# Context projections of a DeltaNet layer: float32 products of unsplit weights in place of three fp32r products of split ones

## The chip, the core and the metric

The kernel runs on one core of one Trainium2 chip. The metric is the device time of one execution in microseconds, as the median of several runs; a lower one is better. The core has TensorE (PE in the rows; its weight loads are PEld), VectorE (DVE), ScalarE (ACT), GpSimd (POOL) and SyncE (SP), which here only issues DMAs. Each engine works through its own list of instructions in order and waits on semaphores.

## The reference, cut to what matters

A layer of a diffusion backbone: gated DeltaNet attention over 512 latent tokens, whose scans start from the final states of scans over 256 context tokens, then a retrieval mixer (PEER) with 128 blocks of 128 experts. D is 1024, there are 8 heads of 128.

```python
hn  = _modulate(_rmsnorm(h, norm_g[i, 0]), sh1, sc1)            # 512 latent tokens
hcn = _modulate(_rmsnorm(hc, norm_g[i, 0]), modc[0], modc[1])   # 256 context tokens
...
z = hn @ w_in                     # the same w_in for both streams
qkv = jax.nn.silu(_short_conv(z[..., :3 * DN_INNER], conv_w, n_rows))
ba = z[..., 4 * DN_INNER:].astype(jnp.float32).reshape(B, L, 2, 2, DN_HEADS)
...
_, sc_f = _gated_delta_chunked(kc, vc, betac[:, 0], gc[:, 0], s0, None)   # context: k, v, decays
o_f, _ = _gated_delta_chunked(k, v, beta[:, 0], g[:, 0], sc_f, q)         # latent, seeded
```

Everything is float32. Of the context only k and v are needed, so its projections are 8 heads of k and 8 of v: a product of a 1024x128 slice of `w_in` with the 1024x256 normed context for each.

## The kernel before, in words

The projections are a list of jobs, one for each head and kind: jobs 0 to 7 are context k (`ck`), 8 to 15 context v (`cv`), and from 16 on the latent q, k, v and gate. A loop over t runs them as a pipeline: in step t it does the projection of job t (`Pj`), the conv taps of job t-1 (`taps`, L353: ACT makes the centre tap, DVE four more, reading the projection from PSUM), transposes and copies of job t-2, fills with pieces of block inverses and norms, splits the weights of job t+2 and loads those of job t+3. Jobs 0 to 3 are done ahead of the loop, chunk by chunk as the context norm comes out (`norm_c`).

A projection multiplies in three fp32r products for each of its 8 chunks of 128 rows. The weight tile `w` (128x1024, 512 KB, DMA by SP) is split into a high part `wh` (cast to fp32r by ACT, L325) and a low part `wl` (`w - wh` by POOL, L326); the normed context is split in the same way into `hcx` high (ACT, L233) and low (DVE, L243). The products are high by high, high by low, low by high (L333), 128x128 weights on 128x256 for the context and on 128x512 for the latent stream. The buffers of `w` are two (WB[0]), those of `wh` and `wl` three each (WB[1]); job 3 splits into two halves in other buffers (`w3`). A projection's result stands in one of two PSUM buffers `pz`; ahead of the loop jobs 2 and 3 use `pk`.

Beside each chunk of the context norm stands a small float32 product for the decays (`aux<-wba,hn`, L247). When its last chunk is done, ACT copies it (`ba`, L260), and a chain of small operations on DVE and ACT makes the decays `g_c`; rows built from them by DVE and POOL (`rw`, L382) go through PE (L396 in fp32r, L399 in float32, both 128x256) into the matrices `Nc`.

Which instruction stands where on an engine is set by the tile framework, which follows the order of the code with priorities, and by buffers that come free. A DMA into a buffer is issued when the last reader of its former content is done.

Of the kernel before, what the change touches and what calls it, by code (L numbers as in the profile page):

```python
# [9 lines left out]
F32 = mybir.dt.float32  # L10
F32R = mybir.dt.float32r
# [4 lines left out]
OP = mybir.AluOpType  # L16
# [4 lines left out]
P = 128  # L21
D = 1024
NC = D // P
TL = 512
TC = 256
H = 8
# [29 lines left out]
WB = (2, 3)  # L56
# [5 lines left out]
NB = {'hn': 4, 'acc': 2, 'ko': 2, 'st': 2}  # L62
# [49 lines left out]
class Trunk:  # L112
# [104 lines left out]
    def norm_rs(self, st, T, rs=None):  # L217
# [3 lines left out]
        nc.vector.reciprocal(rs[:, :T], rs[:, :T])  # L221
        return rs

    def norm_hi(self, src, rs, T, s_, hi, c):
        nc, ma = self.nc, self.ma
        hn = self.tmp("hn", "hn", NB["hn"])
        if NM & (1 + s_):
            nc.vector.scalar_tensor_tensor(hn[:, :T], src[:, c, :], ma[:, c, 1, s_:s_ + 1], rs[:, :T], op0=OP.mult, op1=OP.mult)
            nc.scalar.activation(hi[:, c, :], hn[:, :T], AF.Identity, bias=ma[:, c, 0, s_:s_ + 1])
            return hn  # L230
        (nc.gpsimd if s_ == 0 and c in NP[0] else nc.vector).tensor_tensor(hn[:, :T], src[:, c, :], rs[:, :T], op=OP.mult)
        nc.vector.tensor_scalar(hn[:, :T], hn[:, :T], ma[:, c, 1, s_:s_ + 1], ma[:, c, 0, s_:s_ + 1], op0=OP.mult, op1=OP.add)
        nc.scalar.copy(hi[:, c, :], hn[:, :T])  # L233
        return hn
# [79 lines left out]
        res.update(beta=bt, eG=ex[:, 0], kds=ex[:, 1], gl=ex[:, 2], neg=neg)  # L314


    def w_load(self, src):
        w = self.wp.tile([P, NC, P], F32, name="w", tag="w", bufs=WB[0])
        self.nc.sync.dma_start(w, src)
        return w  # L320

# [7 lines left out]
    def products(self, z, src, w, T):  # L329
        wh, wl = w  # L330
        for c in range(NC):
            for n, (w_, x_) in enumerate(((wh, 0), (wh, 1), (wl, 0))):
                self.nc.tensor.matmul(z[:, :T], w_[c // 4][:, c % 4, :] if isinstance(w_, list) else w_[:, c, :], src[x_][:, c, :], start=c + n == 0, stop=c == NC - 1 and n == 2)  # L333
            yield

    def project(self, src, w, T):
# [266 lines left out]
    def run(self):  # L603
        nc, a, C, mod, ng, dram, tc = self.nc, self.a, self.C, self.mod, self.ng, self.dram, self.tc
        with ExitStack() as tk:
# [43 lines left out]
            for i in (1, 0):  # L649
                nc.vector.tensor_tensor(dg[:, i], C["ident"][:, None, :].to_broadcast([P, NC, P]), self.c2[:, :, i:i + 1].to_broadcast([P, NC, P]),  # L650
                                        op=OP.mult)
# [7 lines left out]
            rsc = self.norm_rs(st_, TC)  # L659
            self.wba = self.cst.tile([P, NC, 32], F32, name="wba")  # L660
            nc.sync.dma_start(self.wba, a["wba"])
            hcx = self.tp.tile([P, 2, NC, TC], F32R, name="hcx", tag="big", bufs=1)
            hc = (hcx[:, 0], hcx[:, 1])
            knc = ub.tile([P, 2, H, P], F32, name="knc")
            vc = ub.tile([P, 2, H, P], F32, name="vc")
            Ncv = Nc.rearrange("p (d t h) i -> p d t h i", d=2, t=2)
# [20 lines left out]
            def load(n):  # L687
                if n < nj:
                    kind, h = jobs[n]
                    ws[n] = self.w_load(a["w_in"][col[kind] + h])  # L690
                elif n < nj + NO:
                    ws[n] = self.w_load(a["w_out"][n - nj])

            def split(n):
                if n < nj + NO:
                    ws[n] = self.w_split(ws[n])

            def Pj(n):
                kind, h = jobs[n]
                g, T, rows, nt = geo(kind)  # L700
                st[n]["z"] = self.project(hc if kind[0] == "c" else hl, ws.pop(n), T)

            def taps(n):
                kind, h = jobs[n]
# [81 lines left out]

            load(0)
            load(1)
            split(0)
            split(1)  # L790
            load(2)
            self.load_params()
            load(3)
            rows = knc.rearrange("p t h d -> p (t h d)")[0:2, :].rearrange("p (i x) -> p i x", x=512)
            bac = self.psum("aux", 1)
            hn = {}
            z0 = [self.pz(), self.pz()]
            pr = []

            def norm_c(cs, last):  # L800
                for c in cs:
                    hn[c] = self.norm_hi(xc, rsc, TC, 1, hc[0], c)
                    if c - 1 in hn:
                        self.norm_lo(hn.pop(c - 1), TC, hc[0], hc[1], bac, c - 1)
                        for p in pr:
                            next(p)
                if last:
                    self.norm_lo(hn.pop(7), TC, hc[0], hc[1], bac, 7)
                    for p in pr:
                        next(p)  # L810
                        next(p, None)

            self.mods_rows(0, ada[0], rows)
            self.mods_rows(1, ada[1], rows)
            self.mods_turn(rows)
            z0.append(self.pk())
            for n in range(3):
                st[n]["z"] = z0[n]
                if n == 2:
                    split(n)  # L820
                pr.append(self.products(z0[n], hc, ws[n], TC))
            norm_c(range(4), False)
            junk = vc.rearrange("p t h d -> p (t h d)")[:, :D]
            self.mods_dots(adaT, cb2, 1, junk)
            norm_c(range(4, 8), True)
            wp = [[self.tmp("w3", "st", NB["st"], (P, 4, P), F32R) for _ in range(2)] for _ in range(2)]
            for i in range(2):
                self.w_split(ws[3][:, 4 * i:4 * i + 4, :], [wp[n][i] for n in range(2)])
            ws[3] = wp
            st[3]["z"] = self.pk()  # L830
            for _ in self.products(st[3]["z"], hc, ws[3], TC):
                pass
            for c in range(NC):
                nc.sync.dma_start(xT[:, c, :], a["xT"][:, c, :])
            load(4)
# [50 lines left out]
            for t in range(1, nj + 3):  # L886
# [57 lines left out]
                        silu(t - 1)  # L944
                with prio("split"):
                    split(t + 2) if t >= 3 else None
                if t == 2:
                    split(4)
                if t <= nj:
                    B(t - 1)  # L950
                mk = []
# [813 lines left out]
```

## Time and profile before

| | |
|---|---|
| median of 3 runs | 1951.41 us (1949.15 to 1956.68) |
| the profiled execution | 1956.64 us |
| its span, first to last instruction | 1954.9 us |
| PE busy over the span | 1819.3 us (93%) |
| DVE busy | 1562.8 us (80%) |
| ACT busy | 855.1 us (44%) |
| POOL busy | 625.6 us (32%) |
| first context product to the last | 41.75 to 151.3 us |
| first latent product | 152.92 us |

Times in the rows are microseconds from the first instruction, means of one instruction are in ns. PE's busy time is modelled from overlapping products, so what a product costs is read from the distance of two starts. A float32 product is recorded as two halves, an fp32r product as one. L12 is line 12 of the kernel.

### The profile page before, as it was taken

What the parts mean: (1) busy time and instruction counts of PE and PEld (TensorE: products, weight loads), DVE (VectorE), ACT (ScalarE), POOL (GpSimd) and SP (SyncE); (2) the same over time, 40 slices, a digit from 0 to 9 for tenths busy, and PEclk for the clock granted to TensorE, in tenths of its full rate; (3) what the DMA queues carried; (4) which work ended last, traced back from release to release, by engine and by line L of the source; (5) the groups of instructions that cost most, each with busy time, mean ns of one, the idle gap of its engine ahead of it and who ended that gap; (6) DMA issues with size and microseconds to landing.
All of it is one profiled execution on the core that took longest, in us unless ns stands there. A gap on an engine that the chain in (4) does not pass through costs nothing.

```text
span 1954.9 us, 29971 instructions
## 1 busy us (share of the span) xinstructions
PE 1819.3 (93%) x11119; PEld 1609.9 (82%) x11119; DVE 1562.8 (80%) x3267; ACT 855.1 (44%) x1399; POOL 625.6 (32%) x395
## 2 busy tenths in 40 slices
PE   7778899878998899799999999999999999999997
PEld 4776788766898887689999888788999998889996
DVE  5998967979388789978999687777777887777885
ACT  3655634523445243247666533333333333333333
POOL 1544412361001133321111022333444443434433
PEclk8888879988799899899999999999999999999998
DMA  8221346424635532147999989999989988989981
GB/s 307 67 87 54 87 130 207 133 86 146 190 114 179 177 98 87 55 162 265 308 316 316 327 292 321 323 346 323 314 311 326 334 304 311 328 304 318 325 275 64
DMA packets 202274, 440.65 MB, mean 225 GB/s; under 512 B 15504, under 2 KB 103696, under 8 KB 198800
## 3 DMA queue, kind: packets, MB, share of 16 engines
q1 hardware_dynamic: 155472, 269.87, 42.5%
q0 software_dynamic: 36864, 134.23, 19.4%
q10 hardware_dynamic: 9792, 34.64, 4.4%
q8 instruction: 87, 1.43, 0.3%
q14 instruction: 59, 0.48, 0.1%
HBM read 388.88 MB, written 49.81 MB: 224 GB/s over the span
## 4 chain that ended last, share of the span: by engine, by line
PE 51%; DVE 11%; DMA 5%; issue 1%; SPq 1%; ACT 0%; DVEq 0%; ACTq 0%
PE pz L1232 25%; PE y L1574 21%; PE py L1509 2%; DMA hTt<-hT_d 2%; DMA ge<-pre_d 2%; DVE wk L1350 1%; PE pz L333 1%; DVE keys L1353 1%; DVE keys L1352 1%; DVE row L1288 1%; DVE keys L1349 1%; DVE keys L1351 1%; DVE wl L1603 1%; DMA keys<-G_d 0%; PE pk L1106 0%
## 5 line engine op out<-in xcount | busy, mean ns | idle before, releaser
L1232 PE MATMUL pz<-hH,wh 128*128 128x384 f32 (+1 forms) x1128 | 391.6, 347 | 2.5 <-ACT small L1253 2.5
L1232 PE MATMUL pz<-hH,wl 128*128 128x384 f32 (+1 forms) x1128 | 389.2, 345 | 0.0
L1232 PE MATMUL pz<-hL,wh 128*128 128x384 f32 (+1 forms) x1128 | 388.8, 345 | 0.0
L1280 POOL DMA_INDIRECT row<-u,small x128 | 169.0, 1320 | 478.3 <-DVE row L1288 456.1
L1597 ACT CAST wh<-w 128x1024 fp32r<-128x1024 f32 x196 | 205.4, 1054 | 181.7 <-PE y L1574 98.0
L1603 DVE TENSOR_TENSOR wl<-w,wh 128x1024 fp32r<-128x1024 f32 x196 | 240.4, 1227 | 46.5 <-ACT wh L1597 46.3
L1280 POOL DMA_INDIRECT row<-v,small x128 | 180.2, 1408 | 223.1 <-DVE small L1296 204.8
L326 POOL TENSOR_TENSOR wl<-w,wh 128x1024 fp32r<-128x1024 f32 x53 | 149.0, 2814 | 294.6 <-ACT wh L325 291.2
L1574 PE MATMUL y<-wh,ch 128*128 128x512 f32 x768 | 238.6, 392 | 2.8 <-ACT ch L1560 2.8
L1574 PE MATMUL y<-wh,cl 128*128 128x512 f32 x768 | 238.0, 391 | 1.8 <-DVE cl L1561 1.8
L1574 PE MATMUL y<-wl,ch 128*128 128x512 f32 x768 | 237.7, 391 | 0.0
L1232 PEld LDWEIGHTS pz<-hH,wh 128*128 128x128 f32 x1128 | 213.6, 189 | 9.5 <-ACT small L1253 2.9
L1232 PEld LDWEIGHTS pz<-hL,wh 128*128 128x128 f32 x1128 | 213.4, 189 | 6.4 <-issue 0.2
L1232 PEld LDWEIGHTS pz<-hH,wl 128*128 128x128 f32 x1128 | 213.2, 189 | 4.3
L1574 PEld LDWEIGHTS y<-wh,cl 128*128 128x128 f32 x768 | 144.2, 188 | 33.4 <-DVE cl L1561 2.8
L1574 PEld LDWEIGHTS y<-wl,ch 128*128 128x128 f32 x768 | 144.5, 188 | 31.4
L1574 PEld LDWEIGHTS y<-wh,ch 128*128 128x128 f32 x768 | 143.5, 188 | 28.9 <-ACT ch L1560 3.5
L1296 DVE SCALAR_TENSOR_TENSOR small<-row,small 128x1024 f32<-128x1024 f32 x127 | 162.6, 1280 | 1.2
L1288 DVE SCALAR_TENSOR_TENSOR row<-row,small 128x1024 f32<-128x1024 f32 x128 | 155.2, 1219 | 0.0
L1253 ACT ACTIVATE ge<-pz 128x384 f32<-128x384 f32 x108 | 53.5, 495 | 214.1 <-PE pz L1232 212.8
L333 PE MATMUL pz<-hlH,wh 128*128 128x512 f32 x256 | 112.4, 439 | 24.4 <-DVE acc L353 19.8
L1516 ACT ACTIVATE keys<-py 128x512 f32<-128x512 f32 x96 | 105.0, 1093 | 55.7 <-PE py L1509 50.8
(477 smaller groups left out, 3361.0 us busy)
## 6 DMA issues: line engine op xcount, KB each, us to landing
w<-uT SPq DMA_DIRECT2D x128, 512.0 KB, 5.0
w<-v SPq DMA_DIRECT2D x128, 512.0 KB, 5.1
w<-w_in SPq DMA_DIRECT2D x48, 512.0 KB, 3.7
G_d<-keys ACTq DMA_DIRECT2D x24, 1024.0 KB, 6.5
adaw<-adaT SPq DMA_DIRECT2D x64, 256.0 KB, 3.4
keys<-G_d SPq DMA_DIRECT2D x8, 1536.0 KB, 13.5
Gt<-G_d SPq DMA_DIRECT2D x8, 1536.0 KB, 13.8
w<-w_q SPq DMA_DIRECT2D x16, 512.0 KB, 3.7
```

Of the source, the lines that this page charges most:

```text
L326: self.last_split = (eng or nc.gpsimd).tensor_tensor(wl, w, wh.bitcast(F32), op=OP.subtract)
L333: self.nc.tensor.matmul(z[:, :T], w_[c // 4][:, c % 4, :] if isinstance(w_, list) else w_[:, c, :], src[x_][:, c, :], start=c + n == 0, st ...
L1232: self.nc.tensor.matmul(out, w[i][:, c, :], x_[:, c, sl], start=c == 0 and n == 0, stop=c == NC - 1 and n == 2)
L1253: self.nc.scalar.activation(ge, z, AF.Gelu)
L1280: nc.gpsimd.indirect_dma_start(out=r, out_offset=None, in_=a["u"] if k < P else a["v"], in_offset=bass.IndirectOffsetOnAxis(ap=self.idx[:, ...
L1288: nc.vector.scalar_tensor_tensor(r, r, 1.0, self.xg, op0=OP.mult, op1=OP.mult, accum_out=self.hid_g[:, k:k + 1])
L1296: nc.vector.scalar_tensor_tensor(self.yg, r, self.coef[:, k:k + 1], self.yg, op0=OP.mult, op1=OP.add)
L1509: nc.tensor.matmul(gp[:, r * P:(r + 1) * P], e[:, 2 + r // 2, :, r % 2], oa[:, 2 * w + r // 2, :, r % 2], start=r == 0 and w == 0, stop=w ...
L1516: nc.scalar.activation(Gs[:, :, i * 4:i * 4 + 4].rearrange("p a t -> p t a"), gps.pop(p).rearrange("p (t a) -> p t a", t=4), AF.Copy, scal ...
L1574: nc.tensor.matmul(yp[2 * t + hf], c_[:, t * P:(t + 1) * P], v_[:, hf * 512:hf * 512 + 512], start=b == 0 and w == 0, stop=b == NBLK - 1 a ...
L1597: nc.scalar.copy(wh, w)
L1603: nc.vector.tensor_tensor(wl, w, wh.bitcast(F32), op=OP.subtract)
```

## The change

The 16 context jobs multiply in float32: one product for each chunk, from the weights as loaded and from the norm as computed. The norm (`norm_whole`) writes float32 straight into `hcx`, without a cast and a subtraction. The weights of the context jobs are not split; they are loaded into the buffers of `w`, `wh` and `wl` in turn (job number modulo 3). Jobs 0 to 3 all go chunk by chunk with the norm. The latent jobs keep their three products, and their splits are as before.

```diff
+    def norm_whole(self, src, rs, h, ba_ps, c):
+        nc, ma = self.nc, self.ma
+        nc.vector.tensor_tensor(h[:, c, :], src[:, c, :], rs[:, :TC], op=OP.mult)
+        nc.vector.tensor_scalar(h[:, c, :], h[:, c, :], ma[:, c, 1, 1:2], ma[:, c, 0, 1:2], op0=OP.mult, op1=OP.add)
+        for t in range(TC // P):
+            nc.tensor.matmul(ba_ps[:, t * 32:(t + 1) * 32], h[:, c, t * P:(t + 1) * P], self.wba[:, c, :], start=c + t == 0,
+                             stop=c == NC - 1, skip_group_check=True)
...
-    def w_load(self, src):
-        w = self.wp.tile([P, NC, P], F32, name="w", tag="w", bufs=WB[0])
+    def w_load(self, src, i=0):
+        w = self.wp.tile([P, NC, P], F32, name="w", tag=("w", "wh", "wl")[i], bufs=WB[i > 0])
...
+    def whole(self, z, src, w):
+        for c in range(NC):
+            self.nc.tensor.matmul(z[:, :TC], w[:, c, :], src[:, c, :], start=c == 0, stop=c == NC - 1)
             yield
...
-            hcx = self.tp.tile([P, 2, NC, TC], F32R, name="hcx", tag="big", bufs=1)
-            hc = (hcx[:, 0], hcx[:, 1])
+            hc = self.tp.tile([P, NC, TC], F32, name="hcx", tag="big", bufs=1)
...
-                    ws[n] = self.w_load(a["w_in"][col[kind] + h])
+                    ws[n] = self.w_load(a["w_in"][col[kind] + h], n % 3 if kind[0] == "c" else 0)
...
-                if n < nj + NO:
+                if 2 * H <= n < nj + NO:
                     ws[n] = self.w_split(ws[n])
...
-                st[n]["z"] = self.project(hc if kind[0] == "c" else hl, ws.pop(n), T)
+                if kind[0] == "c":
+                    st[n]["z"] = self.pz()
+                    for _ in self.whole(st[n]["z"], hc, ws.pop(n)):
+                        pass
+                else:
+                    st[n]["z"] = self.project(hl, ws.pop(n), T)
...
             load(0)
             load(1)
-            split(0)
-            split(1)
             load(2)
...
-            z0 = [self.pz(), self.pz()]
+            z0 = [self.pz(), self.pz(), self.pk(), self.pk()]
...
-                    hn[c] = self.norm_hi(xc, rsc, TC, 1, hc[0], c)
-                    if c - 1 in hn:
-                        self.norm_lo(hn.pop(c - 1), TC, hc[0], hc[1], bac, c - 1)
...
+                    self.norm_whole(xc, rsc, hc, bac, c)
                     for p in pr:
                         next(p)
...
-            for n in range(3):
+            for n in range(4):
                 st[n]["z"] = z0[n]
-                if n == 2:
-                    split(n)
-                pr.append(self.products(z0[n], hc, ws[n], TC))
-            norm_c(range(4), False)
+                pr.append(self.whole(z0[n], hc, ws[n]))
+            norm_c(range(4))
...
-            wp = [[self.tmp("w3", "st", NB["st"], (P, 4, P), F32R) for _ in range(2)] for _ in range(2)]
-            for i in range(2):
-                self.w_split(ws[3][:, 4 * i:4 * i + 4, :], [wp[n][i] for n in range(2)])
...
-                if t == 2:
-                    split(4)
```

On POOL, from its first arithmetic on (`wl` and `w_381` are low parts of weights, `rs` sums for the latent norm, `rw` rows of the context decays), there stood before:

```order
L326 TENSOR_TENSOR wl<-w,wh 128x1024 x3
L326 TENSOR_TENSOR w_381<-w,w_379 128x512
L912 TENSOR_TENSOR rs<-sq 128x512
L912 TENSOR_TENSOR rs<-rs,sq 128x512 x2
L382 TENSOR_TENSOR rw<-cbuf,g_c 128x256 x2
L326 TENSOR_TENSOR w_382<-w,w_380 128x512
L326 TENSOR_TENSOR wl<-w,wh 128x1024
```

And in the changed kernel (its L335 is the split, L397 the rows, L240 a product of the latent norm):

```order
L912 TENSOR_TENSOR rs<-sq 128x512
L912 TENSOR_TENSOR rs<-rs,sq 128x512 x3
L397 TENSOR_TENSOR rw<-cbuf,g_c 128x256 x8
L240 TENSOR_TENSOR hn<-xT,rs 128x512
L335 TENSOR_TENSOR wl<-w,wh 128x1024 x3
```

The sixteen context splits are gone, and the first three that are left belong to latent jobs 16 to 18.

On PE, at the end of the jobs ahead of the loop, there stood before (L247 is the decay projection, `pk<-hcx,w_379` job 3, L304 the sums of the decays):

```order
L247 MATMUL aux<-wba,hn 128x32 x5
L333 MATMUL pk<-hcx,wh 128x256 x2
L247 MATMUL aux<-wba,hn 128x32
L333 MATMUL pz<-hcx,wh 128x256 x2
L247 MATMUL aux<-wba,hn 128x32 x2
L333 MATMUL pk<-hcx,wl 128x256
```

And in the changed kernel (L230 is the decay projection, L348 a float32 product, L916 the sum for the latent norm, L313 the sums of the decays):

```order
L230 MATMUL aux<-wba,hcx 128x32 x2
L348 MATMUL pz<-hcx,w 128x256 x2
L348 MATMUL pk<-hcx,w 128x256 x2
L916 MATMUL aux<-rs,cbuf 128x512
L348 MATMUL pz<-hcx,w 128x256 x5
L313 MATMUL pk<-gd__356,cbuf 128x16
```

The last decay product, which stood ahead of most products of job 2 and of all of job 3, now stands behind all but the last chunk of jobs 0 to 3, and five products of job 4 stand ahead of the sums of the decays.

On DVE, around the copy of the decay projection, there stood before (L243 are low parts of the norm, L267 begins the decays):

```order
L264 TENSOR_SCALAR al<-al 128x16
L232 TENSOR_SCALAR hn<-hn,ma 128x256
L243 TENSOR_TENSOR hcx<-hn,hcx 128x256 x4
L267 TENSOR_TENSOR z__436<-ba__428,dtb 128x32
L268 TENSOR_SCALAR ax__432<-z__436 128x32
```

And in the changed kernel (L228 is the norm, L912 sums for the latent norm, L276 begins the decays):

```order
L228 TENSOR_SCALAR hcx<-hcx,ma 128x256 x2
L273 TENSOR_SCALAR al<-al 128x16
L912 TENSOR_TENSOR rs<-rs,sq 128x512 x3
L276 TENSOR_TENSOR z__328<-ba__320,dtb 128x32
L277 TENSOR_SCALAR ax__324<-z__328 128x32
```

The low parts of the norm are gone, and the three sums of the latent norm, which were spread over the later steps, stand ahead of the decays.

## Rows read from the trace of the kernel before

**Rows 1.** The page: busy us of each engine, share of the span, instructions.

```profile
PE 1819.3 (93%) x11119; PEld 1609.9 (82%) x11119; DVE 1562.8 (80%) x3267; ACT 855.1 (44%) x1399; POOL 625.6 (32%) x395
```

**Rows 2.** Six stretches: us; busy PE, PEld, DVE, ACT, POOL; granted clock; DMA share; GB/s.

```profile
36.20:49.40 13.20, 11.08 (x64) 11.08 (x64) 11.12 (x22) 5.85 (x14) 5.93 (x3) 0.61 0.83 279
49.40:62.10 12.70, 11.34 (x85) 10.79 (x84) 12.32 (x31) 10.45 (x20) 8.26 (x7) 0.92 0.12 45
62.10:89.40 27.30, 17.95 (x111) 15.44 (x109) 27.20 (x34) 15.79 (x32) 17.34 (x12) 0.94 0.29 96
89.40:121.20 31.80, 26.15 (x170) 25.32 (x171) 30.34 (x87) 21.42 (x56) 11.44 (x6) 0.82 0.21 67
121.20:152.90 31.70, 25.53 (x179) 24.23 (x179) 29.79 (x52) 15.60 (x33) 11.59 (x5) 0.89 0.23 76
152.90:199.60 46.70, 39.76 (x156) 30.75 (x157) 41.78 (x70) 27.42 (x38) 20.56 (x16) 0.85 0.16 51
```

**Rows 3.** Waits from 62 to 153 us: total, times, longest.

```profile
POOL wl L326 <- ACT wh L325: 44.4, 10, 14.5
PE pz L333 <- DVE kTc L353: 8.8, 2, 6.4
PE pz L333 <- DVE acc L353: 7.3, 6, 2.1
```

**Rows 4.** Splits and casts, 36 to 153 us: busy, mean ns, idle before.

```profile
L326 POOL TENSOR_TENSOR wl<-w,wh 128x1024 fp32r<-128x1024 f32 x16 | 40.0, 2506 | 53.2 <-ACT wh L325 49.9 <-PE pk L733 3.4
L325 ACT CAST wh<-w 128x1024 fp32r<-128x1024 f32 x15 | 15.6, 1041 | 5.5 <-issue 4.6 <-DMA w<-w_in 0.8
```

**Rows 5.** Timeline of DVE: start, duration, instruction.

```profile
57.12 0.84 DVE L382 TENSOR_TENSOR rw<-cbuf,g_c 128x256 f32<-128x256 f32 x1
...
65.77 2.58 DVE L382 TENSOR_TENSOR rw<-cbuf,g_c 128x256 f32<-128x256 f32 x1
...
101.61 2.33 DVE L417 TENSOR_TENSOR br_c<-bt_c,inv 128x4 f32<-128x4 f32 x1
...
106.21 0.15 DVE L417 TENSOR_TENSOR br_c<-bt_c,inv 128x4 f32<-128x4 f32 x1
...
131.75 0.53 DVE L232 TENSOR_SCALAR hn<-hn,ma 128x512 f32<-128x512 f32 x1
...
134.79 2.62 DVE L232 TENSOR_SCALAR hn<-hn,ma 128x512 f32<-128x512 f32 x1
```

**Rows 6.** Timeline of PE: decay halves, float32 beside fp32r, three fp32r products.

```profile
46.78 1.20 PE L247 MATMUL aux<-wba,hn 128*128 128x32 f32 x10
...
75.98 0.47 PE L396 MATMUL pk<-cr 128*128 128x256 f32 x1
76.29 0.59 PE L399 MATMUL pk<-rw,cr 128*128 128x256 f32 x2
76.53 0.47 PE L396 MATMUL pk<-cr 128*128 128x256 f32 x1
...
78.05 0.40 PE L333 MATMUL pz<-hcx,wh 128*128 128x256 f32 x2
...
78.40 0.40 PE L333 MATMUL pz<-hcx,wh 128*128 128x256 f32 x2
```

**Rows 7.** Timeline of several engines: turning points of the stretch.

```profile
34.47 1.38 DVE L187 SCALAR_TENSOR_TENSOR ma<-ma,ng 128x8 f32<-128x8 f32 x1
...
49.16 0.21 ACT L260 COPY ba__428<-aux 128x64 f32<-128x64 f32 x1 [1.75 <-PE aux L247]
...
59.81 1.85 PE L333 MATMUL pk<-hcx,w 128*128 128x256 f32 x9
...
152.92 0.50 PE L333 MATMUL pz<-hlH,wh 128*128 128x512 f32 x1 [1.06 <-DVE acc L353]
...
163.94 0.77 PE L333 MATMUL pz<-hlH,wh 128*128 128x512 f32 x1 [4.68 <-DVE g_l L288]
```

**Rows 8.** The page: DMA of a weight tile, count, KB, us to landing.

```profile
w<-w_in SPq DMA_DIRECT2D x48, 512.0 KB, 3.7
```

More of the change, by code (lines that the diff above doesn't have):

```diff
@@ L333, in products @@
                 self.nc.tensor.matmul(z[:, :T], w_[c // 4][:, c % 4, :] if isinstance(w_, list) else w_[:, c, :], src[x_][:, c, :], start=c + n == 0, stop=c == NC - 1 and n == 2)
+            yield
+    def whole(self, z, src, w):
+        for c in range(NC):
+            self.nc.tensor.matmul(z[:, :TC], w[:, c, :], src[:, c, :], start=c == 0, stop=c == NC - 1)
             yield
@@ L796, in run, with norm_c @@
             hn = {}
-            z0 = [self.pz(), self.pz()]
+            z0 = [self.pz(), self.pz(), self.pk(), self.pk()]
             pr = []
-            def norm_c(cs, last):
+            def norm_c(cs):
                 for c in cs:
-                    hn[c] = self.norm_hi(xc, rsc, TC, 1, hc[0], c)
-                    if c - 1 in hn:
-                        self.norm_lo(hn.pop(c - 1), TC, hc[0], hc[1], bac, c - 1)
[L805 to L808, printed above, removed]
+                    self.norm_whole(xc, rsc, hc, bac, c)
                     for p in pr:
                         next(p)
-                        next(p, None)
             self.mods_rows(0, ada[0], rows)
@@ L815, in run @@
             self.mods_turn(rows)
-            z0.append(self.pk())
-            for n in range(3):
+            for n in range(4):
                 st[n]["z"] = z0[n]
-                if n == 2:
-                    split(n)
-                pr.append(self.products(z0[n], hc, ws[n], TC))
-            norm_c(range(4), False)
+                pr.append(self.whole(z0[n], hc, ws[n]))
+            norm_c(range(4))
             junk = vc.rearrange("p t h d -> p (t h d)")[:, :D]
             self.mods_dots(adaT, cb2, 1, junk)
-            norm_c(range(4, 8), True)
-            wp = [[self.tmp("w3", "st", NB["st"], (P, 4, P), F32R) for _ in range(2)] for _ in range(2)]
-            for i in range(2):
-                self.w_split(ws[3][:, 4 * i:4 * i + 4, :], [wp[n][i] for n in range(2)])
[L829 to L832, printed above, removed]
+            norm_c(range(4, 8))
             for c in range(NC):
```

## The prediction

> **What bounds the kernel now.** I read the page first, for the busy time by engine; then a table by stretch for the part that the change touches; then, inside it, who waits for whom, and the timelines of VectorE (DVE), GpSimd (POOL) and TensorE (PE). Over the whole span PE is busiest [rows 1], but the change touches only the 16 context jobs, which run from about 36 to 153 us. There the table says something else: from 62.1 to 152.9 us DVE is busy 27.20 + 30.34 + 29.79 = 87.3 of 90.8 us, while PE is busy 77% of it [rows 2]. The waits agree: PE's own waits in that stretch are for DVE's conv taps (8.8 + 7.3 = 16.1 us), and POOL mostly waits for work [rows 3]. So a context job is paid for on DVE.
>
> Not all of DVE's busy time is work. POOL makes the low part of every weight tile, 2.5 us each, 16 whole ones from 36 to 153 us, the last two of them for latent jobs [rows 4]. Where such a split runs, a DVE instruction that reads two SBUF operands, or scales SBUF to SBUF, stands until the split ends: a 128x4 product takes 2.33 us at 101.61, beside 0.15 us at 106.21; a 128x512 scaling takes 2.62 us at 134.79, beside 0.53 at 131.75 [rows 5]. Instructions that take an operand from PSUM (the taps, L353) run through. From 65.77 to 134.79 us ten such stretched instructions lie under context splits, and their times over an unstretched neighbour of the same form are 1.74, 1.77, 2.06, 1.97, 2.18, 1.89, 1.76, 1.18, 1.68 and 2.09 us: 18.3 us in all (first and last, with their neighbours, in [rows 5]).
>
> **The change part by part.**
>
> *Price of a product on PE.* The trace has the new shape: L399 is a float32 product, 128x128 weights on 128x256, recorded as two halves. One fp32r product L396 and one such L399 follow each other every 76.53 - 75.98 = 0.55 us; three fp32r products of 128x256 step by 78.40 - 78.05 = 0.35 us, so one is 0.12 [rows 6]. The float32 product is then 0.55 - 0.12 = 0.43 us and replaces 0.35: +0.08 a chunk, +0.6 us a job, +10 us over 16 jobs of 8 chunks, if PE had no idle time to take it from. The Trainium skill, "FP8 and Floating Point Precision", TensorE Precision Notes, says that true FP32 takes four passes through the array; four against three would make a chunk a third dearer, not a quarter, and as an estimate from that page the 16 jobs would cost about 15 us more (128 chunks by one more pass of 0.12) instead of 10. The rows go into the sum, since they hold what each product costs beside its columns.
>
> *What leaves DVE, ACT and POOL.* 16 splits leave POOL and 16 casts of 1.04 us leave ACT [rows 4]; ACT is under 70% busy in these stretches and POOL waits for work, so by themselves these are worth nothing. Worth something is the 18.3 us that DVE stood under them. Eight low-part subtractions and eight casts of the norm also go; they lie before 49 us, where the front decides.
>
> *The front, 34 to 56 us.* DVE's L187 stands 1.38 us under a split [rows 7] and starts what follows it 1.2 us late; after it four scalings waited likewise. Without splits the first chunk of the norm is on hand near 36.4 us (L187 and its neighbour 0.4, cast of the constants 0.5, two products and one scaling about 0.4 each). From there PE has a dense list: per chunk four jobs at 0.43 and four halves of the decay projection at 0.12 (ten take 1.20 us [rows 6]), 2.2 us, and for eight chunks 17.6 us: 54.0 us. PE is at half clock for much of 36.2 to 49.4 us now (granted 0.61 [rows 2]), while it does a few small products and waits. Bounds: no half clock, 54.0; the same share again, 13.2 x 0.39 = 5.1 us more, 59.1. I take 55.7, nearer the low end, since PE would have full work from the first chunk. Now the fourth job ends at 61.7 [rows 7]: PE is 6 us ahead there. But the last decay product, issued before that chunk's four jobs, moves back: its copy by ACT, now at 49.16 [rows 7], would come 4 x 0.43 = 1.7 us before the end of the front, near 54.0. That chain (decays, then rows and sums) hangs on DVE, which gets idle time in the front.
>
> *DVE from there to the latent jobs.* From 49.4 to 152.9 us DVE is busy 12.32 + 27.20 + 30.34 + 29.79 = 99.7 us and idle 3.9 [rows 2]. Off go 18.3 us of standing and 2.1 us for three sums of the latent norm (L912), which now run ahead of the copy. That leaves 79.3, and 54.0 + 79.3 + 3.9 = 137.2 us for the start of the first latent job, now 152.92 [rows 7].
>
> *PE from there.* Twelve jobs at 8 x 0.43 are 41.3 us, the 16 pairs of L396 and L399 8.8, the rest (latent decay projections, transposes, grams, some 140 halves of 0.12 to 0.13 us) 17.4: 67.5 us at full clock. The mean granted clock of 62.1 to 152.9 is 0.88 [rows 2], which makes 76.7, and 55.7 + 76.7 = 132.4 us. So the two engines come out within 5 us of each other, neither has slack, and each will wait for the other a little more often than now. I add 2 us to the later: 139, a gain of **14 us**. Seen from PE alone: 6 us in front, plus 16.1 us of waits, less 12 x 0.6 = 7.2 us of dearer products, is 15.
>
> *Behind it.* The orders of all engines agree again from about the tenth latent job on, and until then DVE stays nearly full (41.78 of 46.7 us [rows 2]) with the same instructions, so I let the lead pass whole to the end. The weights of latent job 17 can now be asked for only when job 15's last product has left their buffer: 3.7 us to land, 1.04 cast, 2.5 split [rows 4, 8], 7.2 us, against 5.8 us that job 16 keeps PE busy (24 products of 512 columns at twice 0.12). Eleven microseconds lie between the starts of jobs 16 and 17 now (152.92 and 163.94 [rows 7]), for another reason, so I cost this at nothing; without that cover it is 2 us. SP's queue stands meanwhile, with only stores and later loads behind it. On SP the third weight load also moves ahead of the small constants, and the fourth and the latent input no longer wait for splits; the constants are wanted by DVE's first cast in the front and get one load more ahead of them, in a stretch where DVE and PE still wait for the mods, so I cost that at nothing too; if they came late, the front would move with them.
>
> The profiled execution took 1956.64 us, 5.2 above the median of 1951.41. A gain of 14 makes it 1943, and the median **1937 us**.
>
> **The rivals.**
>
> *Half the gain is lost between the engines.* The projection buffer has two places, so each job needs the taps of the job two before; if the taps keep their place in DVE's queue relative to the end of a job, PE's waits don't shrink as DVE frees up, and PE pays its 7.2 us in full. Left is 6 of the front and what of the 18.3 lay directly ahead of a tap; I put the gain at 0 to 9, about 1946 us. For it: both engines come out nearly full. Against it: the waits are put down to those very taps.
>
> *Slower: the granted clock.* At half clock a float32 product costs twice 0.43, and PE has no spare time left to hide it. PE's 67.5 us have 152.9 - 55.7 - 2 = 95 us before the gain is gone; that is a mean clock of 0.71. At 0.61, as in the front stretch, they take 111 us and the first latent job starts near 168: 15 us slower, 1966 us. For it: 0.61 and 0.82 stand in [rows 2]. Against it: PE was partly idle in both, and float32 work fills it.
>
> *More than forecast.* With no half clock in front (end at 54.0, copy at 52.3) and no idle time of DVE behind the copy, 52.3 + 79.3 = 131.6: a gain of 21, 1930 us.
>
> **How the numbers follow.** Forecast, gain of 10 to 21: 0.60. Gain or loss under 0.5% (9.8 us, about what a measurement here tells from no change): 0.30, nearly all of it the first rival. Slower by more: 0.10, the clock, with a small part for the weights of the latent jobs. The range goes from the best bound, 1930, to just short of no change, 1951, which leaves out about 0.15.
>
> **What would show it.** Right: no POOL split before about 130 us; DVE's 128x4 products at 0.15 us throughout; L417, L231 and L232 without instructions over 2 us before the first latent split; the fourth job ending near 56 us and the first latent job starting near 139; a float32 product at 0.43 us at full clock; behind that the same distances as now. Wrong: a first latent job at 148 or later with PE near 95% busy (the first rival, or the clock if the granted share is under 0.75), the lead shrinking between 150 and 500 us, or the copy of the decay projection well after 56 us.

## The result, and the profile after

The changed kernel takes **1927.03 us** (median of 5 runs, 1924.81 to 1939.22) beside 1950.18 us of the kernel before (1939.64 to 1956.68): ratio 0.9889, interval 0.9853 to 0.9924, so 21.6 us faster (14.8 to 28.7). The forecast of 1937 us had the direction and the place right; the gain is half as large again as its 14 us. With the later executions below, twelve of the changed kernel have a median of 1929.9 us. The profiled one took 1939.22 us, its span is 1937.1. One execution of `one_ring_lh9_dve` below took 2544.55 us at a granted clock of 0.65 and is left out of its median.

The page's busy line of the kernel after, to be read against [rows 1]: DVE has 35.1 us less, POOL 37.5, ACT 16.5, and PE only 3.3.

```profile
PE 1816.0 (94%) x10991; PEld 1601.3 (83%) x10991; DVE 1527.7 (79%) x3259; ACT 838.6 (43%) x1374; POOL 588.1 (30%) x378
```

The stretches of the context jobs in the kernel after, from the end of the decay product in front (56.1 us) to the first latent job (132.2), and the one behind; columns as in [rows 2].

```profile
36.40:56.10 19.70, 19.21 (x89) 17.08 (x90) 7.81 (x19) 4.97 (x9) 5.12 (x4) 0.83 0.49 183
56.10:80.50 24.40, 21.26 (x103) 17.87 (x102) 22.06 (x54) 16.41 (x26) 6.76 (x9) 0.93 0.32 108
80.50:106.60 26.10, 24.29 (x140) 21.62 (x141) 25.14 (x98) 15.92 (x61) 0.00 (x0) 1.00 0.19 61
106.60:132.20 25.60, 24.85 (x147) 22.06 (x145) 23.94 (x46) 13.96 (x31) 5.01 (x2) 1.00 0.16 45
132.20:181.00 48.80, 37.82 (x150) 30.06 (x149) 37.70 (x68) 27.22 (x39) 21.04 (x15) 0.83 0.20 63
```

From 56.1 to 132.2 us DVE is busy 22.06 + 25.14 + 23.94 = 71.1 of 76.1 us and PE 70.4, at a mean granted clock of 0.98. Before, the same work and three sums for the latent norm (from 49.4 to 152.9 us in [rows 2]) took DVE 99.7 of 103.5 us. The first latent job starts at 132.27 instead of 152.92 us [rows 7]: 20.7 us earlier, nearly what the median gains. The copy of the decay product, which begins the stretch, and the first latent product after:

```profile
56.06 0.21 ACT L269 COPY ba__320<-aux 128x64 f32<-128x64 f32 x1 [11.39 <-PE aux L230]
...
132.27 0.50 PE L342 MATMUL pz<-hlH,wh 128*128 128x512 f32 x1
```

The timeline of POOL (start, duration, instruction, idle before): after the rows `rw` and one scaling for the norm, no weight is split until job 16's at 121.02.

```profile
73.01 0.62 POOL L397 TENSOR_TENSOR rw<-cbuf,g_c 128x256 f32<-128x256 f32 x1 [0.42 <-PE pk L414]
73.87 1.33 POOL L240 TENSOR_TENSOR hn<-xT,rs 128x512 f32<-128x512 f32 x1 [0.24 <-DVE rs L221]
121.02 2.66 POOL L335 TENSOR_TENSOR wl<-w,wh 128x1024 fp32r<-128x1024 f32 x1 [45.82 <-ACT wh L334]
```

DVE's groups in the kernel before from 49.4 to 152.9 us (busy us, mean ns), those that shrink most and all the small ones named below:

```profile
L179 DVE SCALAR_TENSOR_TENSOR vc<-adaT,cb 128x1024 f32<-128x1024 f32 x8 | 14.2, 1772 | 0.1
...
L382 DVE TENSOR_TENSOR rw<-cbuf,g_c 128x256 f32<-128x256 f32 x8 | 11.9, 1502 | 0.0
...
L232 DVE TENSOR_SCALAR hn<-hn,ma 128x512 f32<-128x512 f32 x8 | 8.0, 1002 | 0.0
L231 DVE TENSOR_TENSOR hn<-xT,rs 128x512 f32<-128x512 f32 x7 | 7.7, 1103 | 0.0
...
L417 DVE TENSOR_TENSOR br_c<-bt_c,inv 128x4 f32<-128x4 f32 x8 | 3.2, 423 | 0.0
...
L279 DVE TENSOR_SCALAR w__445<-u__443 128x32 f32<-128x32 f32 x1 | 1.3, 1251 | 0.0
L313 DVE COPY bt_c<-beta__430 128x32 f32<-128x32 f32 x1 | 1.2, 1192 | 0.0
```

The same groups in the kernel after, 56.1 to 132.3 us:

```profile
L179 DVE SCALAR_TENSOR_TENSOR vc<-adaT,cb 128x1024 f32<-128x1024 f32 x8 | 9.7, 1214 | 0.0
...
L397 DVE TENSOR_TENSOR rw<-cbuf,g_c 128x256 f32<-128x256 f32 x8 | 5.1, 680 | 1.4 <-PE pk L414 1.4
L240 DVE TENSOR_TENSOR hn<-xT,rs 128x512 f32<-128x512 f32 x7 | 4.8, 680 | 0.0
L241 DVE TENSOR_SCALAR hn<-hn,ma 128x512 f32<-128x512 f32 x8 | 4.3, 537 | 0.0
...
L432 DVE TENSOR_TENSOR br_c<-bt_c,inv 128x4 f32<-128x4 f32 x8 | 1.0, 157 | 0.0
```

The counts are the same and the lengths are not: dots 14.2 to 9.7, rows 11.9 to 5.1, scalings of the latent norm 8.0 + 7.7 to 4.3 + 4.8, the 128x4 product 3.2 to 1.0.

PE's timeline in the kernel after gives the price of a float32 product at full clock: a row of 14 halves lasts 3.19 us, one of 16 lasts 3.62, so one product is 0.43 us, as read from [rows 6].

```profile
103.39 3.19 PE L348 MATMUL pz<-hcx,w 128*128 128x256 f32 x14
106.41 0.38 PE L375 MATMUL pw<-cbuf,ko 128*128 128x128 f32 x2
106.63 3.62 PE L348 MATMUL pz<-hcx,w 128*128 128x256 f32 x16
```

### The profile page after: what moved, and what is told of

Its sections match the earlier page's. It is cut to its first block, busy times and chain, and to the rows that moved or that the text cites. A ratio compares the mean times of both kernels' runs of the same rounds, so it can differ in the third digit from the quotient of the medians.

```text
span 1937.1 us, 29649 instructions
## 1 busy us (share of the span) xinstructions
PE 1816.0 (94%) x10991; PEld 1601.3 (83%) x10991; DVE 1527.7 (79%) x3259; ACT 838.6 (43%) x1374; POOL 588.1 (30%) x378
## 4 chain that ended last, share of the span: by engine, by line
PE 52%; DVE 12%; DMA 4%; issue 1%; SPq 0%; ACT 0%; DVEq 0%; ACTq 0%
PE pz L1230 25%; PE y L1572 22%; PE py L1507 2%; DMA ge<-pre_d 2%; DVE wk L1348 1%; DMA hTt<-hT_d 1%; DVE keys L1351 1%; DVE keys L1350 1%; DVE row L1452 1%; PE pz L342 1%; DVE keys L1347 1%; DVE keys L1349 1%; DVE row L1286 1%; DMA keys<-G_d 0%; PE pk L1104 0%
## 5 line engine op out<-in xcount | busy, mean ns | idle before, releaser
L335 POOL TENSOR_TENSOR wl<-w,wh 128x1024 fp32r<-128x1024 f32 x38 | 113.0, 2976 | 259.6 <-ACT wh L334 243.2
L1514 ACT ACTIVATE keys<-py 128x512 f32<-128x512 f32 x96 | 104.9, 1092 | 55.7 <-PE py L1507 50.9
```

The source lines that it names most:

```text
L335: self.last_split = (eng or nc.gpsimd).tensor_tensor(wl, w, wh.bitcast(F32), op=OP.subtract)
L1514: nc.scalar.activation(Gs[:, :, i * 4:i * 4 + 4].rearrange("p a t -> p t a"), gps.pop(p).rearrange("p (t a) -> p t a", t=4), AF.Copy, scal ...
```

## The experiments

The theory is that the gain is DVE's standing under POOL's passes over the context weights. The rivals are the rest of the change: the unsplit norm and the denser front, the weights ordered earlier into more buffers, ACT's casts, and the products on PE. Each run below was timed beside the kernel before on the same chip.

**POOL's passes put back (`dummy_split`).**

```diff
 def split(n):
-    if 2 * H <= n < nj + NO:
+    if n < 2 * H:
+        nc.gpsimd.tensor_tensor(ws[n], ws[n], C["ones"][:, None, :].to_broadcast([P, NC, P]), op=OP.mult)
+    elif n < nj + NO:
         ws[n] = self.w_split(ws[n])
```

(called for the context jobs where before called `split`)

> The kernel after, with a GpSimd pass over each of the 16 context weight tiles put back where the low part was made (a product with ones, written in place, so the products and their operands stay the same; the ScalarE cast stays away). Theory (the gain is VectorE's standing under GpSimd's passes over the weights): VectorE's instructions of two SBUF operands in the context jobs stand about 1.7 us again, ten or so of them, the first latent job starts 14 to 20 us later than the 132.3 us of the kernel after, and the median is 1939 to 1948 us. Rival (the front without a split norm, or weights ordered earlier, made the gain): no more than 4 us are lost, 1927 to 1931 us. Rival (ScalarE's casts made it): likewise no loss, since none comes back.

Measured: 1949.18 us (12 runs), ratio to before 0.9996 (0.9973 to 1.002); first latent job at 151.1 us. The whole gain is gone, 1 us beyond the theory's range, with unsplit norm, float32 products and three pairs of buffers all in place. No wait of PE from 36 to 151 us ends with one of the new passes. DVE's timeline shows three of the instructions that stand:

```profile
59.39 2.24 DVE L277 TENSOR_SCALAR ax__328<-z__332 128x32 f32<-128x32 f32 x1
63.49 2.26 DVE L289 TENSOR_TENSOR w__341<-e__327,w__341 128x32 f32<-128x32 f32 x1
93.10 2.98 DVE L179 SCALAR_TENSOR_TENSOR vc<-adaT,cb 128x1024 f32<-128x1024 f32 x1
```

The first two take 0.18 us each in the kernel after, and they lie on the chain of the decays: PE, done with the front's products at 60.7 us, later waits 5.89 us for that chain's `lu` (2.55 at the same product in the kernel after) and then for taps behind the stretched dot (start, duration, idle before):

```profile
67.44 4.60 PE L348 MATMUL pz<-hcx,w 128*128 128x256 f32 x10 [5.89 <-DVE lu__340 L294]
...
100.75 1.22 PE L348 MATMUL pz<-hcx,w 128*128 128x256 f32 x2 [5.26 <-DVE kTc L368]
...
102.19 5.27 PE L348 MATMUL pz<-hcx,w 128*128 128x256 f32 x14
```

After the second wait its granted clock is 0.61 for 7 us, in which 14 halves take 5.27 us instead of the 3.19 above, and 1.00 behind that:

```profile
95.00:101.00 6.00, 0.74 (x6) 0.63 (x6) 6.00 (x11) 0.79 (x3) 2.93 (x2) 0.88 0.14 55
101.00:108.00 7.00, 7.00 (x25) 5.69 (x26) 3.56 (x20) 1.86 (x9) 0.00 (x0) 0.61 0.01 2
108.00:120.00 12.00, 12.00 (x68) 10.74 (x67) 11.71 (x56) 7.16 (x20) 0.14 (x1) 1.00 0.13 44
```

From the time of the copy in the kernel after to its own first latent job, the run with the passes has:

```profile
56.10:151.10 95.00, 80.48 (x405) 68.53 (x403) 84.23 (x197) 46.46 (x117) 37.73 (x22) 0.89 0.19 57
```

DVE is busy 84.2 us, 13.1 more than in the kernel after, and idle 10.8, 5.8 more; together these are the 19 us by which the first latent job is late. So the stands cost more than their own length here: DVE also waits for a copy that comes at 58.92 instead of 56.06, and for PE in the slow stretch.

**Low parts left out of before (`before_no_low`).**

```diff
+if not low:
+    nc.scalar.copy(wh, w)
+    return wh, wh
...
-ws[n] = self.w_split(ws[n])
+ws[n] = self.w_split(ws[n], low=n >= 2 * H)
```

> The kernel before with the GpSimd low part of the 16 context weights left out; its third product takes the high part again, so TensorE does as many products, the split norm, the weight casts and the two weight buffers stay as before (the low part of the context weights is missing from the result). Theory: the 18 us that VectorE stands are gone and the products cost 0.35 us a chunk and not 0.43, so the first latent job starts at 132 to 138 us and the median is 1928 to 1935 us. Rival (the front, the unsplit norm or the early weights made the gain): the time stays within 4 us of the kernel before, 1946 to 1954 us.

Measured: 1938.06 us (7 runs), ratio 0.9938 (0.9915 to 0.9961), 12 us faster; first latent job at 137.2 us, inside the theory's range, the total 3 us above it. From the copy of the decay product to there, as from 49.4 to 152.9 us in [rows 2]:

```profile
49.40:137.20 87.80, 74.75 (x508) 69.81 (x507) 75.79 (x205) 63.59 (x137) 15.85 (x14) 0.88 0.29 87
```

DVE is busy 75.8 us where it was 99.7. The other 12.0 us DVE is idle; PE, with the cheaper products, is granted 0.88 there and not 0.98. Whether that clock or the waits for the casts cost the last 5 us was not taken apart.

**Low parts on DVE in before (`before_ctx_dve`).**

```diff
-ws[n] = self.w_split(ws[n])
+ws[n] = self.w_split(ws[n], None, nc.vector if n < 2 * H else None)
```

(the two halves of job 3 likewise)

> The kernel before with the low parts of the 16 context weights made on VectorE; split norm, casts, products and buffers as before. Twelve subtractions of about 1.25 us behind the front put 15 us on VectorE, and the stretched instructions of the context jobs, 26.6 us over their lengths in the kernel after, go back to their own lengths. Theory (standing is what cost): first latent job 8 to 12 us earlier than 152.9, at 141 to 145 us, median 1938 to 1944 us. Rival (the work moved to VectorE eats it): 150 to 155 us, median 1948 to 1953 us.

Measured: 1932.67 us (6 runs), ratio 0.9899 (0.9872 to 0.9925), about as much as the whole change wins, though DVE took on the work. The first latent job starts at 148.7 us here and at 143.8 in a second trace, one outside the theory's range and one in it: 8 us ahead of the kernel before in the mean (146.3 beside 154.5 of three traces, below), where the change has 21 to 23. DVE's groups from 49.4 us to there: 12 subtractions cost 14.6 us, the rows are at 4.7, the 128x4 products at 0.9.

```profile
L326 DVE TENSOR_TENSOR wl<-w,wh 128x1024 fp32r<-128x1024 f32 x12 | 14.6, 1219 | 0.4 <-ACT wh L325 0.4
...
L382 DVE TENSOR_TENSOR rw<-cbuf,g_c 128x256 f32<-128x256 f32 x8 | 4.7, 610 | 2.5 <-PE pk L399 1.5 <-issue 1.0
...
L417 DVE TENSOR_TENSOR br_c<-bt_c,inv 128x4 f32<-128x4 f32 x8 | 0.9, 158 | 0.0
```

The lead fits the theory in the mean; the total lies 5 us under the theory's range and is better than the lead, see the same kernels again below.

**Half the products (`half_products`).**

```diff
 for c in range(NC):
-    self.nc.tensor.matmul(z[:, :TC], w[:, c, :], src[:, c, :], start=c == 0, stop=c == NC - 1)
+    if c % 2 == 0:
+        self.nc.tensor.matmul(z[:, :TC], w[:, c, :], src[:, c, :], start=c == 0, stop=c == NC - 2)
```

> The kernel after with only four of the eight chunks of each context product (half of the context projections' sum is left out). TensorE has 64 x 0.43 = 27.5 us less to do in 16 jobs, 6.9 of them in the front. If VectorE sets the pace of the context jobs, only the front's share comes through: first latent job 5 to 8 us earlier, at 124 to 127 us. If TensorE, 93 to 97% busy in the kernel after, sets it, 15 to 25 us come through, at 108 to 117 us. In the total about 7 us are given back at the latent decays in either case, if that chain and not the products sets the pace of jobs 16 to 18.

Measured: 1927.76 us (4 runs), ratio 0.9893 (0.9866 to 0.992), the same as the kernel after. Job 4 starts 9.5 us earlier, the first latent job 5.1 (127.2 us, 0.2 beyond the range for a pace set by DVE and 10 from the range for one set by PE). The stretches, to compare with those of the kernel after:

```profile
56.10:80.50 24.40, 18.77 (x84) 16.43 (x84) 20.28 (x40) 14.86 (x20) 6.98 (x9) 0.79 0.24 92
80.50:106.60 26.10, 19.45 (x100) 16.57 (x100) 23.85 (x95) 17.86 (x64) 0.00 (x0) 0.80 0.06 21
106.60:127.20 20.60, 16.75 (x81) 13.71 (x82) 19.95 (x44) 11.67 (x24) 2.35 (x1) 0.83 0.16 51
```

So PE's products do not set the pace of the context jobs; DVE does. PE is busy 55.0 of these 71.1 us at a granted clock of about 0.80, where the kernel after has 70.4 of 76.1 at 0.98.

**ACT's casts put back (`dummy_cast`)**: as `dummy_split`, with `nc.scalar.copy(ws[n], ws[n])` in place of the GpSimd product.

> The kernel after with a ScalarE copy over each of the 16 context weight tiles (in place, so nothing changes in the values), where the cast of the split stood; GpSimd does nothing with them. Theory (ScalarE has time left in the context jobs, GpSimd's passes were the cost): 0 to 3 us lost, first latent job at 132 to 136 us, median 1925 to 1931 us. Rival (the casts queue ahead of ScalarE's taps and hold TensorE, so they were a third of the gain): 5 to 8 us lost, first latent job at 137 to 140 us, median 1932 to 1936 us.

Measured: 1934.83 us (6 runs), ratio 0.9915 (0.9886 to 0.9945), beside 1931.83 us and 0.9904 (0.9873 to 0.9935) of the kernel after, measured with it; first latent job at 131.5 us, and from job 20 to 43 its starts lie within about 0.1 us of the second trace of the kernel after. The median alone lies in the rival's range, but the kernel after itself stands at the edge of it, and the intervals overlap; the first latent job, 131.5 us beside the rival's 137 to 140, decides against the rival. No cost of the casts shows here.

**One pair of buffers (`one_ring`)**

```diff
-ws[n] = self.w_load(a["w_in"][col[kind] + h], n % 3 if kind[0] == "c" else 0)
+ws[n] = self.w_load(a["w_in"][col[kind] + h], 0)
```

> The kernel after with all context weights loaded into the two buffers of the unsplit weights alone, not into the three pairs in turn. Theory (the third and further buffers only order weights earlier than they are wanted): a job's weights are asked for when the job two before it has finished, some 4 us before they are wanted in the densest stretch, beside 3.7 us for the transfer, so 0 to 3 us are lost; in the front, where four jobs run side by side, the third and fourth weights come only when the first two are done, which costs the front 4 to 8 us of its own, first latent job at 136 to 144 us, median 1930 to 1938 us. Rival (early weights count for nothing even there): first latent job at 132 to 134 us.

Measured: 1925.13 us (6 runs), ratio 0.9867 (0.9834 to 0.99). The expected delay of the front is there (job 5 at 76.7 us beside 67.5), but it is gone by job 8 (93.7 beside 93.8) and the first latent job starts at 130.6: the theory's ranges for it and for the median were wrong. The copy of the decay product comes 5 us earlier (50.73 beside 56.06), since two jobs less stand beside it, and DVE's chain runs while PE catches up. So loading the weights into the parts' buffers in turn, the change's own addition to the queue, is worth nothing measurable.

**The latent norm one job earlier (`lh9`)**: `LH = 9` in place of 10.

> The kernel after with the latent norm's statistics, its norm and the latent decays one job earlier (LH 9 in place of 10). Theory (the 7 us that jobs 16 to 18 gave back were lost to the chain of the latent decays, rows and sums): job 18 starts up to 6 us earlier than 165.5, and the median is 3 to 6 us under that of the kernel after, 1921 to 1924 us. Rival (the work of these jobs is full on VectorE whatever its order): the context jobs get longer by what the latent ones win, and the median stays within 2 us of 1927, or above it.

Measured: 1929.59 us (6 runs), ratio 0.9897 (0.9875 to 0.992), no different from the kernel after. Job 18 starts at 159.9 us, 5.6 earlier than in the first trace of the kernel after (2.0 earlier than in its second), but job 16 at 136.7, 4 to 6 later. The lead at job 18 is not worth anything in the total; the rival holds.

**The latent weights' low parts on DVE (`split_dve`, and with LH 9)**

```diff
-ws[n] = self.w_split(ws[n])
+ws[n] = self.w_split(ws[n], None, nc.vector if n < nj else None)
```

> The kernel after with the latent norm and decays one job earlier (LH 9), and the low parts of the latent weights of w_in made on VectorE and not on GpSimd. If VectorE's standing under GpSimd's passes is the same cost in the latent jobs, each pass of GpSimd that stretches one instruction by 1.7 to 2.6 us becomes one of 1.2 us on VectorE: 0.5 to 1 us a job where VectorE sets the pace, up to 10 us in all over LH 9 alone, 1917 to 1926 us. Rival (VectorE does not set the pace from job 20 on, so the extra 1.2 us a job only load it): the time stays at that of LH 9 alone, 1926 to 1932 us, or above.

> The kernel after with the low parts of the latent weights of w_in made on VectorE and not on GpSimd, LH 10 as in after: which half of the pair before made the 14.7 us. Theory (GpSimd's passes cost VectorE more than the subtraction itself, in the latent jobs as in the context jobs): 8 to 14 us below the kernel after, 1917 to 1923 us. Rival (the earlier latent norm made it, or both are needed): 1926 to 1932 us.

Measured: with LH 9, 1917.12 us, ratio 0.9829 (0.9799 to 0.9858); alone 1912.54 us, ratio 0.98 (0.9764 to 0.9837), so LH 9 is not needed and **this one edit beats both kernels**: its interval lies below that of the kernel after, and its median 4 us below the theory's range. Jobs 16 to 28 take 124.4 us (132.2 to 256.6) beside 147 to 155 in three traces of the kernel after; of these, jobs 16 to 25, ahead of a stretch whose length changes between executions (below), take 84.2 beside 95.4 to 99.6. DVE's groups from 130 to 300 us, first in the kernel after (its second trace):

```profile
L397 DVE TENSOR_TENSOR rw<-cbuf,gL 128x512 fp32r<-128x512 f32 x16 | 17.2, 1077 | 2.0 <-PE aux L414 1.9
L474 DVE TENSOR_TENSOR invT<-inv 128x31 f32<-128x31 f32 (+15 forms) x31 | 16.8, 541 | 3.3 <-POOL inv L467 2.7
L477 DVE TENSOR_TENSOR inv<-inv,invT 128x31 f32<-128x31 f32 (+15 forms) x31 | 14.8, 478 | 0.6
```

and in `split_dve`:

```profile
L335 DVE TENSOR_TENSOR wl<-w,wh 128x1024 fp32r<-128x1024 f32 x16 | 20.3, 1267 | 0.6 <-ACT wh L334 0.6
L474 DVE TENSOR_TENSOR invT<-inv 128x31 f32<-128x31 f32 (+15 forms) x31 | 14.4, 463 | 0.7 <-POOL inv L467 0.6
L397 DVE TENSOR_TENSOR rw<-cbuf,gL 128x512 fp32r<-128x512 f32 x16 | 13.7, 854 | 1.5 <-PE aux L414 1.4
L477 DVE TENSOR_TENSOR inv<-inv,invT 128x31 f32<-128x31 f32 (+15 forms) x31 | 12.8, 413 | 0.2
```

DVE takes on 20.3 us and these three groups give back 7.9, so DVE is busier; what falls besides is waits (DVE's `acc` taps for ACT, over 57 and 66 of them, 7.7 and 3.0 us; its `qa` and `v` products for PE likewise). Which wait is worth most was not taken apart.

**Combinations**: LH 9, one pair of buffers and the low parts on DVE (`one_ring_lh9_dve`), then the output weights on DVE too (`one_ring_lh9_dve_out`).

> The kernel after with three edits: context weights through one pair of buffers, LH 9, low parts of the latent weights on VectorE. Theory (no single stretch but the total of VectorE's standing and of TensorE's idle time counts, and the one pair of buffers only moves the front): 1912 to 1918 us. Rival (the one pair's apparent 6 us were scatter between executions): 1916 to 1921 us, as with the other two alone.

> The same with the low parts of the output weights on VectorE too. If GpSimd's passes cost VectorE there as well: 2 to 6 us less than the run before, 1908 to 1915 us. If VectorE, 150 us busy of the 200 between 300 and 500 us, has time for standing there: the same time within 2 us.

Measured: 1915.86 us (5 runs), ratio 0.9812 (0.9784 to 0.984), and 1918.32 us (5 runs), 0.9828 (0.98 to 0.9856). Neither beats `split_dve`; the first falls at the edge of both ranges and decides nothing, the second is 2.5 us above it, half a microsecond outside what DVE having time to stand later on was to give, and not faster as the other answer had it.

**The same kernels again.** One timed repeat of the kernel after, then four single executions.

> The kernel after once more, unchanged, on the chip of the runs beside it, for a second trace and more runs. Of its first trace two things may be the kernel or that one execution: the lead shrank by 7 us in jobs 16 to 18 (granted clock 0.83 there) and its time was 12 us above the four others of the kernel. If the give-back belongs to the order of instructions, the first latent job starts near 132 and job 18 near 165 us again, and job 27 near 274; if it belongs to the clock of that execution, job 27 starts up to 7 us earlier. Median 1924 to 1932 us.

> The kernel before, unchanged, for a second trace. If the times of jobs 25 to 28 (52.6 us, granted clock 0.81) and of the stretch of 54.3 us behind 620 us (0.91) belong to the execution and not to the kernel, one of them differs by 5 us or more here, at another clock; the first latent job starts within 2 us of 152.9. If they belong to the kernel, all three come back within 2 us.

> The same, for a third trace: if the two stretches belong to the execution, three traces of the kernel before spread over 5 us or more in at least one of them.

> The kernel before with the context low parts on VectorE once more: its median is 17.5 us below the kernel before, but its first latent job only 4.2 us earlier, and 15.5 us were won in the two stretches with a changing clock. If those belong to the execution, jobs 25 to 28 or the stretch behind 620 us are 5 us or more longer here than 43.4 and 48.0 us. If they belong to the kernel, both come back within 2 us. The first latent job starts at 147 to 151 us either way.

> The kernel after, for a third trace: first latent job at 130 to 133 us; jobs 25 to 28 (55.5 and 48.9 us so far) and the stretch behind 620 us (48.2 and 55.9 us) at other lengths again if the execution decides them.

Measured: 1931.83 us (6 runs), ratio 0.9904 (0.9873 to 0.9935), for `after_again`; the single executions, in the order above, took 1950.34, 1943.31, 1925.26 and 1938.99 us. Job 27 starts at 264.2 us in the second trace of the kernel after, not at 274 as in the first, so that difference belongs to the execution. Starts and lengths in us (the fourth column is one stretch of work, named by its times in the first trace of the kernel after):

| trace | job 16 | jobs 16 to 25 | jobs 25 to 28 | about 608 to 656 | span |
|---|---|---|---|---|---|
| before | 152.9, 154.9, 155.8 | 95.1, 95.4, 97.6 | 52.6, 52.6, 47.0 | 54.3, 48.0, 48.1 | 1954.9, 1948.6, 1941.5 |
| after | 132.3, 130.3, 132.2 | 99.6, 98.5, 95.4 | 55.5, 48.9, 55.5 | 48.2, 55.9, 55.7 | 1937.1, 1927.8, 1936.9 |
| low parts on DVE in before | 148.7, 143.8 | 97.1, 99.1 | 43.4, 43.4 | 48.0, 48.4 | 1935.4, 1923.5 |

The start of job 16 belongs to the kernel: 22.9 us between the means, three traces of each within 3 us. The two later stretches differ by 5.6 to 7.7 us between executions of one kernel, before and after alike. Their granted clock goes with the length: 0.78 to 0.93 in the first, 0.88 to 0.96 in the second. For the kernel with the low parts on DVE, jobs 25 to 28 are short in both executions (0.96 both times), so its extra gain there may be its own; why stays open.

## Why the prediction was right and where it failed

**The place and the mechanism were right.** The context jobs were paid for on DVE. With POOL's passes back, the gain is gone. With them taken out of before, much of it appears without the rest of the change: of the 22.9 us at job 16, 17 when they are left out, and 8 when DVE makes the low parts itself in 14.6 us. The Trainium skill, "SBUF — State Buffer", section "SBUF: two separate sides", calls the port pair that VectorE and GpSimd share an exclusive lock, held for a whole instruction. The traces agree in kind: a 128x32 scaling of 0.18 us takes 2.24 beside a POOL pass.

**The step that failed: "the 18.3 us that DVE stood".** This term was too small. DVE is relieved of 99.7 - 71.1 = 28.5 us; 2.1 of them are the three sums that I had moved ahead, and 26.4 are standing. Three things were left out. The neighbour that I took as unstretched, 0.84 us for L382 [rows 5], stood itself: the eight rows fall from 11.9 to 5.1 us, of which I had counted 3.5. I began at 65.77 us, and so missed L279 and L313, which fall from 2.5 us to under 0.4. The remaining 2.7 us or so are smaller stretches. With the measured terms the same sum gives 56.1 + 71.1 + 5.0 = 132.2, where I had 54.0 + 79.3 + 3.9 + 2. The best bound of the range, 52.3 + 79.3, was built from the same term.

Not all of the 26.4 us stood under passes over weights. L313 and L279 stood under POOL's sums for the latent norm (L912), in the kernel before:

```profile
50.62 1.30 POOL L912 TENSOR_TENSOR rs<-sq 128x512 f32<-128x512 f32 x1 [1.68 <-ACT sq L211]
51.99 1.29 POOL L912 TENSOR_TENSOR rs<-rs,sq 128x512 f32<-128x512 f32 x1
...
50.76 1.19 DVE L313 COPY bt_c<-beta__430 128x32 f32<-128x32 f32 x1
...
52.07 1.25 DVE L279 TENSOR_SCALAR w__445<-u__443 128x32 f32<-128x32 f32 x1
```

With two of the rows, at 55.23 and 70.04 us, that is about 4 us which the change won by moving those sums ahead of the copy, and not by dropping the splits; about 21 us stood under context weights. That move was not tried by itself, but `dummy_split` keeps it and gains nothing.

**The front came later than said**: the copy at 56.06 us, not 54.0; the other two traces have it at 54.81 and 56.52. The difference passes on: in the three traces job 16 starts 75.4 to 76.2 us after the copy, and in the three of the kernel before 103.8 to 104.0 us after it. So the stretch behind the copy is 28 us shorter, and a copy that comes 5 us later in the mean takes 5 of them back. `half_products`, with the copy 6 us earlier, has the first latent job 5.1 us earlier; `one_ring`, with PE still behind, only 1.7.

**The product's price was right, its consequence not.** 0.43 us a product is what the trace shows. But I took PE's 67.5 us at the mean clock of before, 0.88, and PE got 0.98. That PE's own sum, 132.4, lies at the measured start is luck: the front ended later and the clock was higher than it says. The rival of a clock under 0.71 was on the wrong side: PE was busy 92% of the stretch and its clock rose. `half_products`, with 27.5 us less on PE, was granted 0.80, and its total is the same. The Trainium skill's four passes ("FP8 and Floating Point Precision", TensorE Precision Notes) would be 4 x 0.117 = 0.47 us by the fp32r price in [rows 6], an estimate; the rows give 0.43.

**The rivals.** Half the gain lost between the engines: no, PE's waits for taps fell from 16.1 us to 2.4 in the same stretch. ACT was not under 70% busy throughout, as I had it: from 49.4 to 62.1 us it was 10.45 of 12.70 [rows 2]; `dummy_cast` shows that nothing hung on it. More than forecast, 1930 us: nearest in time, but by another way. It needed a front without half clock and DVE without idle time; the clock of the front was 0.83 and DVE idled 5.0 us.

**"The lead passes whole to the end"** is not shown. The medians over all runs of the kernel after differ from before by about 20 us, close to the 22.9 at job 16, but the mean spans of the three traces of each only by 14.4. Jobs 16 to 18 take 33.3, 31.7 and 30.5 us in the three traces of the kernel after and 25.8 to 26.0 in those of before: 4.5 to 7.5 us are given back there. In the first trace PE waits 4.6 us for taps there, 2.7 for ACT's `ko`, 2.2 for rows of the latent decays on POOL and 1.4 for the decays themselves, 10.9 in all where it had waited 5.8; which of them decides was not taken apart. It is not the weights of job 17, which I had costed at nothing: their split ends at 130.7 us. All but 1.8 us in the mean has returned by job 25, and `lh9`, which moves the chain of the latent decays, wins nothing. The rest is in stretches that change between executions of one kernel: each of the two in the table by up to 6.6 and 7.7 us, and the work between them (from job 28 on) by 5 to 6 more, for a reason that stays open. One pair of traces can't show a lead behind them, and the 17.8 us between the first profiled spans are such a pair.

## What to carry to other kernels

Where POOL works through large tiles in SBUF, compare the lengths of DVE's SBUF-to-SBUF instructions with the shortest of the same form anywhere in the trace, not with a neighbour, and count all of them from the first pass on. Work that POOL does beside a full DVE can be worth moving to DVE even if DVE is then busier. And before a difference behind the changed stretch is explained, look at two traces of one kernel.

## What the runs showed of the hardware

In jobs 25 to 28 one program takes 55.5 or 48.9 us. From 252 to 274 us PE is busy throughout in both of these traces of the kernel after. It works through the same list in the same order, some 3 us further on in the second, and does 262 instructions in one and 347 in the other:

```profile
252.00:274.00 22.00, 22.00 (x262) 19.68 (x259) 10.07 (x32) 8.62 (x23) 2.35 (x1) 0.54 0.32 98
```

```profile
252.00:274.00 22.00, 22.00 (x347) 18.98 (x346) 8.89 (x29) 12.92 (x29) 3.13 (x2) 0.95 0.31 98
```

The granted clock is 0.54 in the first and 0.95 in the second, though the engine was as full. The same instructions, from a row of 64 products of 32x32 to the start of job 27, take 17.6 us in the first (256.3 to 273.9) and 11.2 in the second (253.0 to 264.2). From 240 to 252 us, ahead of it, PE had been busy 8.1 and 8.5 of 12 us. I had not expected a run-to-run difference of 7 us from one such place in a kernel whose starts agree within 3 us up to job 16.
